# Decays of a gated linear attention made in place, level by level, and its scan begun at the keys

## The chip, the cores and the metric

The kernel runs on one core of one Trainium2 chip. Its time is device time in microseconds (us), of the one core; three runs stand for it and their median is the figure used. The engines are named as in the profile: PE (TensorE: matmuls), PEld (its weight loads), DVE (VectorE), ACT (ScalarE), POOL (GpSimd), SP (SyncE, which issues most transfers here). PE writes into PSUM, of which the kernel uses eight banks of 128 x 512 float32: three called `pj`, three `pt`, two `pc`.

## What is computed

One layer of a decoder trunk over 16 meta tokens and 2048 real ones of width 1024. From the normed input `u` one wide projection gives the inputs of two branches, an SSD branch (16 heads in 4 groups, chunks of 128) and a gated linear attention (4 heads, keys of 128, values of 256), and the gates that merge them; a branch projection and an output projection follow. The change lies in the linear attention. Cut to its core:

```python
q = q.reshape(b, l, GLA_HEADS, GLA_HEAD_K) * (GLA_HEAD_K ** -0.5)
gate_logit = jnp.einsum('blr,rk->blk', a_lr, gla_gate_w2) + gla_gate_b
log_a = jax.nn.log_sigmoid(gate_logit) / GLA_GATE_TEMP          # per token and key channel
gc = jnp.cumsum(to_chunks(log_a), axis=3)                       # within a chunk
def step(s, inp):
    qi, ki, vi, gi = inp
    o_inter = jnp.einsum('bhtk,bhkv->bhtv', qi * jnp.exp(gi), s)
    rel = gi[:, :, :, None, :] - gi[:, :, None, :, :]
    rel = jnp.exp(jnp.where(causal, rel, -jnp.inf))
    att = jnp.einsum('bhtk,bhsk,bhtsk->bhts', qi, ki, rel)
    o_intra = jnp.einsum('bhts,bhsv->bhtv', att, vi)
    k_dec = ki * jnp.exp(g_last[:, :, None, :] - gi)
    s_new = jnp.exp(g_last)[..., None] * s + jnp.einsum('bhsk,bhsv->bhkv', k_dec, vi)
    return s_new, o_inter + o_intra
```

The decay between a query at t and a key at s is different for each key channel, so `att` is not one matmul with a mask. The kernel (chunks of 128 tokens) takes it in levels: for a block of 2h tokens, the queries of its second half meet the keys of its first half, and the decay splits into a factor on the query's side and one on the key's side. Levels h = 64, 32, ... and the diagonal fill the lower triangle.

## The kernel before

The real tokens are four blocks of 512 (`BLK`). For each block the first half of the program projects eight units from `u` (`uh`, `ul`, a high and a low part): four SSD groups (`ssd_proj`), then four attention heads (`gla_proj`). Every large product is split into three matmuls (`accum`, lines 183 to 187). A head of `gla_proj` (line 605) projects queries, keys, values (two halves) and two output gates, each about one step; after every step `step()` (line 828) advances all generators that have been begun by one `yield`. So a scan's work lies on PE behind the projections of the next units, in an order written out by hand (`manual_schedule` for PE and SP, line 842). The order on DVE, ACT and POOL is planned by the tile scheduler, as is the order on PE in the second half.

`gates` (line 414) makes the log decays of all four heads of a block and, in line 445, their running sums inside each chunk, into `g_all`. `gla_scan` (line 644) is begun after a head's output gates; for the last head of the last block already after the values, and then the keys are turned later (`last`). It first makes the decayed keys `kd` (lines 660, 661) and the decayed queries `qg` (665, 666). `level_in(half)` (line 675) then makes, in tiles of its own, the two operands of a level: the running sum minus its value at the middle of the block (688), two exponentials (691, 692), times the keys (693) and, in two pieces, times the queries (695). The result `kq` is laid out so that both operands are contiguous. `level_out(half)` (line 699) multiplies them, two matmuls of 128 x 128 in plain float32 into a `pc` bank (line 703), and copies what belongs to that level into `xa` under a mask (line 710). A level's operands are made one to two levels ahead. Pairs of neighbours (level 1) and the diagonal are made by sums over channels with a matrix of ones (lines 751 to 776). `xa` holds two chunks in one tile: one in its upper, the other in its lower triangle, and lines 778 to 791 part them and turn one by a transpose (790). Then, chunk by chunk (796 to 806), values and state are applied, the state `s_gla` is carried on (802), and the output is normed, turned (816), gated (817) and stored (820).

The second half (from line 868) multiplies by the gate, branch and output weights, each product in seven partial ones (`product`, `PS`). Its first four products are put between the last steps of the first half (`between`, lines 1114 to 1123). Its operands are loaded and split on ACT and DVE (`prep_b`, lines 903 and 904; `prep_a`, 928 and 929), into memory that the first half gives back: one part when the projections have ended (`inputs.close()`), the rest when the scans have (`first.close()`).

Of the kernel before, what the change touches and what calls it, by code (L numbers as in the profile page):

```python
# [14 lines left out]
P = 128  # L15
# [6 lines left out]
GH = 4  # L22
# [5 lines left out]
NACT = 8  # L28
NC1 = 6
LEVELS = (64, 32, 16, 8, 4, 2)  # L30
NMSK = len(LEVELS) + 1
# [9 lines left out]
def trunk_kernel(ctx: ExitStack, tc: tile.TileContext, xm, xmt, w_feat, w_tok, w_zm, w_br, w_o,  # L41
# [85 lines left out]
    def bank(pool, tag):  # L127
        return mk(pool, [P, 512], F32, tag)

# [107 lines left out]
    def load_u(b):  # L237
# [54 lines left out]
        for kt in range(KT):  # L292
            xk = mk(wk, [P, META + BLK], F32, "act" if m0 else "acc", bufs=NACT if m0 else 2)[:, :tt]
# [38 lines left out]
    def late_constants():  # L332
        w2r = mk(wk, [P, META + BLK], F32, "act", bufs=NACT)[:48, :512]
# [11 lines left out]
    def new_block(b, u):  # L345
# [13 lines left out]
        o.g_all = mk(bpool, [P, GH, META + BLK], F32, "g_all")  # L359
        o.alr = mk(bpool, [P, 5, 48], F32, "alr")  # L360
# [53 lines left out]
    def gates(o):  # L414
        m0, tt, chunks, g_all = o.m0, o.tt, o.chunks, o.g_all
        ast = mk(wk, [P, META + BLK], F32R, "act", bufs=NACT)[:48, :tt]
# [10 lines left out]
        for h2 in range(0, GH, 2):  # L427
# [14 lines left out]
            for h in (h2, h2 + 1):  # L442
                nc.vector.tensor_tensor(gmt[:, h % 2, :tt], gmt[:, h % 2, :tt], g_all[:, h, :tt], op=ALU.subtract)
                for a, n in chunks:
                    nc.vector.tensor_tensor_scan(g_all[:, h, a:a + n], ones[:, :n], gmt[:, h % 2, a:a + n], 0.0,
                                                 op0=ALU.mult, op1=ALU.add)
                yield


    def ssd_proj(o, g):  # L450
# [16 lines left out]
        for j in range(4):  # L467
# [13 lines left out]
            f = mk(wk, [P, META + BLK], F32, "act", bufs=NACT)  # L481
# [123 lines left out]
    def gla_proj(o, h):  # L605
        m0 = o.m0
        t0 = T_GLA + 4 * h
        qs = mk(wk, [P, META + BLK], F32, "act", bufs=NACT)
        ps, = proj_feat(f"g{t0}", w_feat[t0], o.segs_real, o.mov)
        nc.scalar.activation(qs[:, :BLK], ps, AF.Copy, scale=QSCALE)  # L610
        yield
        kf = mk(wk, [P, META + BLK], F32, "act", bufs=NACT)
        for ps, (a, n) in zip(proj_feat(f"g{t0 + 1}", w_feat[t0 + 1], o.segs_all, o.mov), o.segs_all):
            nc.scalar.activation(kf[:, a:a + n], ps[:, :n], AF.Copy)
        yield
        vh = mk(wk, [P, NCH, 256], F32R, "tok4", bufs=NT4)
# [8 lines left out]

        last, gs = (o.b, h) == (nblk - 1, GH - 1), []
        if last:
            begin(gla_scan(o, h, qs, kf, (vh, vl), vm, gs, True))
        if m0:
            nc.scalar.activation(vm, pv5[:META, :256], AF.Copy)  # L630
        for r, ps in enumerate(pss):
            split(*[t[:, 2 * r:2 * r + 2].rearrange("p c f -> p (c f)") for t in (vh, vl)], ps)
        yield
        for j in range(2):
# [4 lines left out]
            gs.append(gg)  # L639
            yield  # L640
        if not last:
            begin(gla_scan(o, h, qs, kf, (vh, vl), vm, gs))

    def gla_scan(o, h, qs, kf, vt, vm, gs, last=False):
        m0, tt = o.m0, o.tt
        gf = o.g_all[:, h, :tt]
        gr = gf[:, m0:]
        q = qs[:, :BLK]
        k = kf[:, m0:tt]
        grc = gr.rearrange("p (c t) -> p c t", t=P)  # L650

        kd = mk(wk, [P, META + BLK], F32, "act", bufs=NACT)
        gl = mk(sm, [P, NCH + 1], F32, "gl")
        nc.scalar.activation(gl[:, :NCH], grc[:, :, P - 1], AF.Copy, scale=ITEMP)
        if m0:
            nc.scalar.activation(gl[:, NCH:], gf[:, META - 1:META], AF.Copy, scale=ITEMP)
            nc.scalar.activation(kd[:, :META], gf[:, :META], AF.Exp, scale=-ITEMP, bias=gl[:, NCH:])
        for c in range(NCH):
            cs = slice(m0 + c * P, m0 + (c + 1) * P)
            nc.scalar.activation(kd[:, cs], gf[:, cs], AF.Exp, scale=-ITEMP, bias=gl[:, c:c + 1])  # L660
        nc.vector.tensor_tensor(kd[:, :tt], kd[:, :tt], kf[:, :tt], op=ALU.mult)
        egl = mk(sm, [P, NCH], F32, "egl")
        nc.scalar.activation(egl, gl[:, :NCH], AF.Exp)
        qg = mk(wk, [P, META + BLK], F32, "act", bufs=NACT)[:, :BLK]
        nc.scalar.activation(qg, gr, AF.Exp, scale=ITEMP)
        nc.vector.tensor_tensor(qg, qg, q, op=ALU.mult)

        xa = mk(wk, [P, 2, P], F32, "c1", bufs=NC1)
        kqs = {}

        def level_in(half):
            nb = BLK // (2 * half)
            npc = P // (2 * half)

            def view(t):
                return t.rearrange("p (b two h) -> p b two h", two=2, h=half)  # L680

            def view5(t):
                return t.rearrange("p (r o b two h) -> p r o b two h", o=2, b=npc, two=2, h=half)

            ex = mk(wk, [P, BLK], F32, "sq", bufs=NSQ)
            kq = mk(wk, [P, BLK], F32, "sq", bufs=NSQ)
            ev = view(ex)
            nc.vector.tensor_tensor(
                ex.rearrange("p (b s) -> p b s", s=2 * half), gr.rearrange("p (b s) -> p b s", s=2 * half),
                view(gr)[:, :, 0, half - 1:half].to_broadcast([P, nb, 2 * half]), op=ALU.subtract)  # L690
            nc.scalar.activation(ev[:, :, 0], ev[:, :, 0], AF.Exp, scale=-ITEMP)
            nc.scalar.activation(ev[:, :, 1], ev[:, :, 1], AF.Exp, scale=ITEMP)
            nc.vector.tensor_tensor(view(kq)[:, :, 0], ev[:, :, 0], view(k)[:, :, 0], op=ALU.mult)
            for i in range(2):
                nc.vector.tensor_tensor(view5(kq)[:, :, 1 - i, :, 1], view5(ex)[:, :, i, :, 1],
                                        view5(q)[:, :, i, :, 1], op=ALU.mult)
            kqs[half] = kq

        def level_out(half):
            kq = kqs.pop(half)  # L700
            ps = bank(pc, "pc")
            for r in range(2):
                nc.tensor.matmul(ps[:, r * P:(r + 1) * P], kq[:, 2 * r * P:(2 * r + 1) * P],
                                 kq[:, (2 * r + 1) * P:(2 * r + 2) * P], start=True, stop=True)
            pv2 = ps[:, :256].rearrange("p (r t) -> p r t", t=P)
            if half == 64:
                nc.scalar.activation(xa, pv2, AF.Copy)
            else:
                mi = msk[:, LEVELS.index(half)].unsqueeze(1).to_broadcast([P, 2, P])
                nc.vector.copy_predicated(xa, mi, pv2)  # L710

        level_in(64)
        yield
        if m0:
            ps = bank(pt, "pt")
            nc.tensor.transpose(ps[:META, :P], kd[:, :META], ident)
            btm = mk(wk, [P, P], F32, "bt")
            nc.scalar.activation(btm[:META], ps[:META, :P], AF.Copy)
        kdt = []

        def turn_keys():
            ps = bank(pt, "pt")
            for c in range(NCH):
                nc.tensor.transpose(ps[:, c * P:(c + 1) * P], kd[:, m0 + c * P:m0 + (c + 1) * P], ident)
            kdt.extend(mk(wk, [P, NCH, P], F32R, "kdt", bufs=2) for _ in range(2))
            split(*[t.rearrange("p c t -> p (c t)") for t in kdt], ps)

        if not last:
            turn_keys()
        level_in(32)  # L730
        level_out(64)
        level_in(16)
        yield
        if m0:
            ps = bank(pc, "pc")
            nc.tensor.matmul(ps[:, :256], btm[:META], vm, start=True, stop=True)
            nc.vector.tensor_copy(s_gla[:, h], ps[:, :256])
        level_out(32)
        level_in(8)
        level_out(16)  # L740
        level_in(4)
        yield
        level_out(8)
        level_in(2)
        level_out(4)


        def halves(t):
            return t.rearrange("p (r o b two) -> p r o b two", o=2, b=P // 2, two=2)

        pn = mk(wk, [P, 2, P // 2, 2], F32, "c1", bufs=NC1)
        for i in range(2):
            eo = pn[:, :, :, 1 - i]
            nc.vector.tensor_tensor(eo, halves(gr)[:, :, i, :, 1], halves(gr)[:, :, i, :, 0], op=ALU.subtract)
        nc.scalar.activation(pn, pn, AF.Exp, scale=ITEMP)
        for i in range(2):
            eo = pn[:, :, :, 1 - i]
            nc.vector.tensor_tensor(eo, eo, halves(q)[:, :, i, :, 1], op=ALU.mult)
            nc.vector.tensor_tensor(eo, eo, halves(k)[:, :, i, :, 0], op=ALU.mult)
        pd = mk(wk, [P, BLK], F32, "sq", bufs=NSQ)  # L760
        nc.vector.tensor_tensor(pd, q, k, op=ALU.mult)
        parts = []
        for src, n, tg, nb in ((pn.rearrange("p r b o -> p (r b o)"), 256, "c1", NC1), (pd, BLK, "sq", NSQ)):
            hl = [mk(wk, [P, n], F32R, tg, bufs=nb) for _ in range(2)]
            split(*hl, src)
            parts.append((hl, n))
        yield
        level_out(2)
        sums_ = []
        for hl, n in parts:  # L770
            ps = bank(pt, "pt")
            for i in range(2):
# [460 lines left out]
```

## Time and profile before

| | us |
|---|---|
| median of three runs | 2326.85 |
| the runs | 2323.31, 2326.85, 2329.19 |
| the profiled execution, its span | 2327.3 |
| busy PE, PEld | 2247.1, 1956.3 |
| busy DVE, ACT, POOL | 1550.3, 1184.8, 684.6 |

The profiled execution is known by its span alone, from its first to its last instruction; no time outside the span is given for it. Matmuls are pipelined: the start of one to the start of the next tells what it costs, the duration of one is longer. A float32 matmul shows as two records, each with its weight load; so four records of line 703 are one level. "[2.59 <-ACT junk L806]" behind an instruction of a timeline is the time its engine stood idle before it and what ended that. In a group's row stand the instruction's line, engine and operation, what it writes and reads, the count, then the busy time, the mean ns of one, and the idle time before it with its cause.

### The profile page before, as it was taken

To read this page: it belongs to the slowest core of one execution; us is meant where nothing else is said; L and a number is where in the kernel's file an instruction comes from. 1 tells how busy PE (TensorE), PEld (TensorE's weight loads), DVE (VectorE), ACT (ScalarE), POOL (GpSimd) and SP (SyncE) were. 2 spreads that over 40 slices of the span, in tenths; PEclk is the share of its full clock that TensorE was granted. 3 is DMA by queue.
4 is the path that set the end of the run, shared out by engine and by line. 5 is a ranking of instruction groups with operands and counts; after the bars stand their busy time and mean duration, and the time that the engine had idled before them with its cause. 6 is when DMAs were issued, how large, how long until landed. Compare 5 with 4: busy or idle time off the path is not lost. (4 is left out here: it accounts for less than half of the span.)

```text
span 2327.3 us, 36519 instructions
## 1 busy us (share of the span) xinstructions
PE 2247.1 (97%) x12641; PEld 1956.3 (84%) x12641; DVE 1550.3 (67%) x2895; ACT 1184.8 (51%) x2758; POOL 684.6 (29%) x681
## 2 busy tenths in 40 slices
PE   7899999999999999999999999889999999999998
PEld 7899888888888989898988898768888888888776
DVE  5676766676675666566568555654588954788766
ACT  4666655465544455544465443554554545554443
POOL 3344433122221122212122100037324264324331
PEclk9999999999999999999999999989999999999999
DMA  8766865767785666786677655457577866687743
GB/s 302 230 204 208 292 228 205 223 199 237 244 284 181 214 213 217 255 270 215 194 230 214 206 168 162 145 178 247 186 255 268 305 227 216 231 286 259 243 145 122
DMA packets 301545, 518.05 MB, mean 223 GB/s; under 512 B 27696, under 2 KB 143664, under 8 KB 301360
## 3 DMA queue, kind: packets, MB, share of 16 engines
q1 hardware_dynamic: 200400, 402.84, 53.0%
q10 hardware_dynamic: 100960, 112.88, 14.1%
q8 instruction: 99, 1.62, 0.3%
q14 instruction: 86, 0.70, 0.1%
HBM read 368.42 MB, written 147.19 MB: 222 GB/s over the span
## 5 line engine op out<-in xcount | busy, mean ns | idle before, releaser
L185 PE MATMUL pj<-u,whl 128*128 128x512 f32 (+1 forms) x1184 | 449.0, 379 | 14.6 <-ACT acc L475 6.7
L187 PE MATMUL pj<-u,whl 128*128 128x512 f32 (+1 forms) x1184 | 433.5, 366 | 1.4 <-POOL whl L166 0.8
L186 PE MATMUL pj<-u,whl 128*128 128x512 f32 (+1 forms) x1184 | 432.0, 365 | 0.0
L185 PE MATMUL pj<-whl,u 128*128 128x256 f32 (+1 forms) x992 | 289.0, 291 | 2.4 <-ACT u L298 1.5
L187 PE MATMUL pj<-whl,u 128*128 128x256 f32 (+1 forms) x992 | 282.4, 285 | 1.6 <-DVE u L300 1.6
L186 PE MATMUL pj<-whl,u 128*128 128x256 f32 (+1 forms) x992 | 282.2, 284 | 1.0 <-POOL whl L166 1.0
L185 PEld LDWEIGHTS pj<-u,whl 128*128 128x128 f32 x1184 | 226.8, 192 | 53.7 <-ACT acc L475 7.7
L185 PE MATMUL pj<-b,a 128*128 128x512 f32 x640 | 254.0, 397 | 13.8 <-ACT sn L945 7.6
L187 PEld LDWEIGHTS pj<-u,whl 128*128 128x128 f32 x1184 | 226.0, 191 | 38.0 <-POOL whl L166 1.9
L186 PEld LDWEIGHTS pj<-u,whl 128*128 128x128 f32 x1184 | 227.0, 192 | 33.6
L187 PE MATMUL pj<-b,a 128*128 128x512 f32 x640 | 252.2, 394 | 0.0
L186 PE MATMUL pj<-b,a 128*128 128x512 f32 x640 | 251.0, 392 | 0.0
L185 PEld LDWEIGHTS pj<-whl,u 128*128 128x128 f32 x992 | 189.7, 191 | 4.0 <-ACT u L298 1.8
L187 PEld LDWEIGHTS pj<-whl,u 128*128 128x128 f32 x992 | 189.6, 191 | 2.3 <-DVE u L300 2.3
L80 POOL TENSOR_TENSOR wr<-wr 128x256 f32<-128x256 f32 x80 | 66.3, 829 | 425.0 <-DMA wr<-u 174.7
L186 PEld LDWEIGHTS pj<-whl,u 128*128 128x128 f32 x992 | 189.9, 191 | 1.6 <-POOL whl L166 1.2
L166 POOL TENSOR_TENSOR whl<-wr,whl 128x512 fp32r<-128x512 f32 (+1 forms) x100 | 134.7, 1355 | 187.4 <-ACT whl L165 151.5
L904 DVE TENSOR_TENSOR b<-br,b 128x512 fp32r<-128x512 f32 x196 | 154.9, 808 | 44.7 <-ACT b L903 43.5
L919 POOL TENSOR_TENSOR as<-ar,ar 128x512 f32<-128x512 f32 x40 | 60.0, 1499 | 411.3 <-DMA ar<-in_w_br 197.3
L479 DVE SCALAR_TENSOR_TENSOR acc<-cin,hcw,acc 128x512 f32<-128x512 f32 (+1 forms) x192 | 154.4, 804 | 30.9 <-ACT acc L475 29.8
L929 DVE TENSOR_TENSOR a<-ar,a 128x512 fp32r<-128x512 f32 x160 | 126.3, 797 | 67.2 <-ACT a L928 64.4
L903 ACT ACTIVATE b<-br 128x512 fp32r<-128x512 f32 x196 | 119.4, 626 | 99.0 <-DMA br<-br_t 38.6
(274 smaller groups left out, 5068.8 us busy)
## 6 DMA issues: line engine op xcount, KB each, us to landing
whl<-k_s SPq DMA_DIRECT2D x96, 512.0 KB, 4.5
whl<-k_g SPq DMA_DIRECT2D x96, 512.0 KB, 4.2
whl<-k_v SPq DMA_DIRECT2D x48, 512.0 KB, 3.7
whl<-k_z SPq DMA_DIRECT2D x36, 512.0 KB, 3.8
wr<-in_w_feat SPq DMA_DIRECT2D x64, 256.0 KB, 4.5
k_s<-whl SPq DMA_DIRECT2D x32, 512.0 KB, 3.6
cb<-cumd ACTq DMA_DIRECT2D x64, 256.0 KB, 5.8
y<-gg ACTq DMA_DIRECT2D x64, 256.0 KB, 4.5
```

What stands on the lines that cost most here:

```text
L80: nc.gpsimd.tensor_tensor(o, x, y, op=ALU.subtract)
L166: nc.gpsimd.tensor_tensor(hl[:, 1], raw, hl[:, 0].bitcast(F32), op=ALU.subtract)
L185: nc.tensor.matmul(ps, sh, mh, start=first, stop=False, **kw)
L186: nc.tensor.matmul(ps, sh, ml, start=False, stop=False, **kw)
L187: nc.tensor.matmul(ps, sl, mh, start=False, stop=last, **kw)
L479: nc.vector.scalar_tensor_tensor(acc, cin[:, k:k + tt], hcw[:, ti, k:k + 1], acc, op0=ALU.mult, op1=ALU.add)
L903: nc.scalar.activation(t[:, 0], raw, AF.Copy)
L904: nc.vector.tensor_tensor(t[:, 1], raw, t[:, 0].bitcast(F32), op=ALU.subtract)
L919: nc.gpsimd.tensor_tensor(s1, a21, a22, op=ALU.add)
L929: nc.vector.tensor_tensor(t[:, 1], src, t[:, 0].bitcast(F32), op=ALU.subtract)
```

## The change

- `gates` leaves the log decays themselves in `g_all`; the running sums inside a chunk are gone.
- Keys and queries of a head are halves of one tile (`pair_tile`, four of two rows each in place of eight single ones; other users of that pool take halves too). The scan is begun right after the keys' projection (`gla_keys`); the values and the output gates come into lists that the scan reads later.
- The scan sums the log decays over blocks of 2, 4, ... 128 tokens, and takes the exponentials of all of them at once. It starts with queries that carry their own token's decay, and goes from level 1 up to level 64. After a level, `level(half)` multiplies keys and queries in place: the keys of a block's first half and the queries of its second half by the exponential of the other half's sum. After level 64 they are the keys decayed to the chunk's end and the queries decayed from its start, which `kd` and `qg` were.
- A level's stationary operand is packed by ACT into a tile of its own (`pack`); the moving operand is read with strides straight from the pair tile (`odd_even`), in runs of `half` elements that alternate between keys and queries. There are seven levels by matmul; the sums over channels remain for the diagonal alone. The chunks that share `xa` are now 0 with 2 and 1 with 3.
- In the last block, the keys of head 3 are projected before the output gates of head 2. A scan has fourteen steps where it had eleven.
- Tile counts: `NACT` 8 to 4 (of double size), `NC1` 6 to 7.

```diff
-NACT = 8
-NC1 = 6
-LEVELS = (64, 32, 16, 8, 4, 2)
+NACT = 4
+NC1 = 7
+LEVELS = (1, 2, 4, 8, 16, 32, 64)
...
+    def pair_tile(dt=F32):
+        return mk(wk, [P, 2, META + BLK], dt, "act", bufs=NACT)
...
-                nc.vector.tensor_tensor(gmt[:, h % 2, :tt], gmt[:, h % 2, :tt], g_all[:, h, :tt], op=ALU.subtract)
-                for a, n in chunks:
-                    nc.vector.tensor_tensor_scan(g_all[:, h, a:a + n], ones[:, :n], gmt[:, h % 2, a:a + n], 0.0,
-                                                 op0=ALU.mult, op1=ALU.add)
+                nc.vector.tensor_tensor(g_all[:, h, :tt], gmt[:, h % 2, :tt], g_all[:, h, :tt], op=ALU.subtract)
...
+    def gla_keys(o, h):
+        kq = pair_tile()
         ps, = proj_feat(f"g{t0}", w_feat[t0], o.segs_real, o.mov)
+        nc.scalar.activation(kq[:, 1, m0:m0 + BLK], ps, AF.Copy, scale=QSCALE)
+        yield
         for ps, (a, n) in zip(proj_feat(f"g{t0 + 1}", w_feat[t0 + 1], o.segs_all, o.mov), o.segs_all):
+            nc.scalar.activation(kq[:, 0, a:a + n], ps[:, :n], AF.Copy)
+        o.gla[h] = [], []
+        begin(gla_scan(o, h, kq, *o.gla[h]))
+        yield
...
+    def gla_proj(o, h):
+        ahead = o.b == nblk - 1 and h >= GH - 2
+        if not ahead or h == GH - 2:
+            yield from gla_keys(o, h)
+        yield from gla_values(o, h)
+        if ahead and h == GH - 2:
+            yield from gla_keys(o, GH - 1)
+        yield from gla_out_gates(o, h)
...
+        def odd_even(half, start, nb, skip):
+            pitch = list(kq.ap[0])
+            return bass.AP(kq.tensor, kq[:, 0, start:].offset, [pitch, [2 * half, nb], [skip, 2], [1, half]])
...
+        while n > NCH:
+            n //= 2
+            dst = ex[:, at:at + n]
+            two = src.rearrange("p (b two) -> p b two", two=2)
+            nc.vector.tensor_tensor(dst, two[:, :, 0], two[:, :, 1], op=ALU.add)
+            place[BLK // n] = (at, n)
+            src, at = dst, at + n
+        nc.scalar.activation(ex[:, :BLK], la, AF.Exp, scale=ITEMP)
+        nc.scalar.activation(egl, src, AF.Exp, scale=ITEMP)
+        nc.scalar.activation(ex[:, BLK:at - NCH], ex[:, BLK:at - NCH], AF.Exp, scale=ITEMP)
+        nc.vector.tensor_tensor(pd, q, k, op=ALU.mult)
+        nc.vector.tensor_tensor(q, q, ex[:, :BLK], op=ALU.mult)
...
+        def pack(half):
+            packed[0] = mk(wk, [P, 2 * P], F32, "c1", bufs=NC1)
+            nb = P // half
+            nc.scalar.activation(packed[0].rearrange("p (b two h) -> p b two h", two=2, h=half),
+                                 odd_even(half, m0, nb, k_to_q + 2 * P + half), AF.Copy)
+
+        def level(half):
             ps = bank(pc, "pc")
             for r in range(2):
+                nc.tensor.matmul(ps[:, r * P:(r + 1) * P], packed[0][:, r * P:(r + 1) * P],
+                                 odd_even(half, m0 + (r + 2) * P, P // (2 * half), k_to_q - 2 * P + half),
+                                 start=True, stop=True)
...
+            nb = BLK // (2 * half)
+            kv = odd_even(half, m0, nb, k_to_q + half)
+            at = place[half][0]
+            other = bass.AP(ex.tensor, ex[:, at + 1:].offset, [list(ex.ap[0]), [2, nb], [-1, 2], [0, half]])
+            nc.vector.tensor_tensor(kv, kv, other, op=ALU.mult)
+            if half < P // 2:
+                pack(2 * half)
```

More of the change, by code (lines that the diff above doesn't have):

```diff
@@ L292, in load_u @@
         for kt in range(KT):
-            xk = mk(wk, [P, META + BLK], F32, "act" if m0 else "acc", bufs=NACT if m0 else 2)[:, :tt]
+            if not m0:
+                xk = mk(wk, [P, META + BLK], F32, "acc")[:, :tt]
+            else:
+                if kt % 2 == 0:
+                    two = pair_tile()
+                xk = two[:, kt % 2, :tt]
             nc.sync.dma_start(xk, xmt[:, kt, row0:row0 + tt])
@@ L638, in gla_proj @@
             nc.vector.scalar_tensor_tensor(gg, gg, 1.0, ps, op0=ALU.add, op1=ALU.mult)
-            gs.append(gg)
+            o.gla[h][1].append(gg)
             yield
-        if not last:
-            begin(gla_scan(o, h, qs, kf, (vh, vl), vm, gs))
-    def gla_scan(o, h, qs, kf, vt, vm, gs, last=False):
-        m0, tt = o.m0, o.tt
[L646 to L654, printed above, removed]
-        if m0:
[L656 to L666, printed above, removed]
-        xa = mk(wk, [P, 2, P], F32, "c1", bufs=NC1)
[L673 to L700, printed above, removed]
@@ L715, in gla_scan @@
             ps = bank(pt, "pt")
-            nc.tensor.transpose(ps[:META, :P], kd[:, :META], ident)
+            nc.tensor.transpose(ps[:META, :P], km, ident)
             btm = mk(wk, [P, P], F32, "bt")
             nc.scalar.activation(btm[:META], ps[:META, :P], AF.Copy)
[L719 to L732, printed above, removed]
+        level(2)
+        yield
+        level(4)
         yield
@@ L760, in gla_scan @@
[L760 to L772, printed above, removed]
-                nc.tensor.matmul(ps[:, :n], ones_r, hl[i], start=i == 0, stop=i == 1)
-            sums_.append(ps)
@@ L775, in gla_scan @@
-        nc.vector.copy_predicated(xa, msk[:, len(LEVELS)].unsqueeze(1).to_broadcast([P, 2, P]),
-                                  sums_[0][:, :256].rearrange("p (r t) -> p r t", t=P))
+        level(16)
+        yield
+        level(32)
+        pdt = [mk(wk, [P, BLK], F32R, "sq", bufs=NSQ) for _ in range(2)]
+        split(*pdt, pd)
+        yield
+        level(64)
+        diag = bank(pt, "pt")
+        for i in range(2):
+            nc.tensor.matmul(diag, ones_r, pdt[i], start=i == 0, stop=i == 1)
@@ L1189, in _layout @@
     cmsk[:, 0] = np.eye(P)
-    for i, h in enumerate(LEVELS + (1,)):
+    for i, h in enumerate(LEVELS):
         if i:
```

89 lines of the change are left out of this document (47 added, 42 removed).

## The prediction

> **What bounds the kernel now.** I read the page's busy shares first, then the busy times by stretch, then what TensorE (PE) waited for, then PE's timeline where the stretches show a hole.
>
> ```profile
> PE 2247.1 (97%) x12641; PEld 1956.3 (84%) x12641; DVE 1550.3 (67%) x2895; ACT 1184.8 (51%) x2758; POOL 684.6 (29%) x681
> ```
>
> PE is busy 97% of a span of 2327.3 us. The profiled execution is 0.45 us above the median shown (2326.85), so a sum made against the span may be read against the median. Only 80 us of PE idle time exist, and what the change takes from VectorE (DVE) and ScalarE (ACT) is worth nothing but the part of those 80 us that it frees. So I need to know where they lie.
>
> ```profile
> 965.00:1012.00 47.00, 43.53 (x270) 38.69 (x269) 29.48 (x69) 26.16 (x74) 12.60 (x17) 1.00 0.78 260
> ...
> 1190.00:1240.00 50.00, 49.73 (x299) 42.95 (x298) 37.31 (x77) 32.35 (x78) 11.28 (x17) 1.00 0.67 204
> ...
> 1367.00:1407.00 40.00, 40.00 (x246) 35.84 (x245) 20.12 (x50) 14.04 (x33) 1.76 (x2) 1.00 0.52 169
> ...
> 1450.00:1494.00 44.00, 44.00 (x275) 39.45 (x274) 26.65 (x71) 20.51 (x57) 2.19 (x1) 1.00 0.38 125
> 1494.00:1523.00 29.00, 18.82 (x89) 15.42 (x88) 24.29 (x50) 16.45 (x43) 8.59 (x6) 0.76 0.50 164
> 1523.00:1536.00 13.00, 13.00 (x65) 10.95 (x64) 2.90 (x6) 6.05 (x19) 3.56 (x4) 1.00 0.00 0
> 1536.00:1550.00 14.00, 7.90 (x27) 6.12 (x26) 9.95 (x15) 7.61 (x14) 1.22 (x1) 0.76 0.73 249
> ```
>
> Columns: stretch, its length, then busy PE, PEld, DVE, ACT, POOL, the granted clock, DMA. The first four are linear-attention heads and one SSD group; PE hardly stops there. From 1494 to 1550, between the last input projection and the steady products of the second half, PE idles 16 us and the granted clock falls to 0.76, while DVE is busy 24.29 of 29 us.
>
> ```profile
> PE pt L790 <- DVE sq L781: 6.8, 2, 4.4
> PE pj L185 <- ACT acc L475: 6.7, 5, 4.3
> PE pc L801 <- DVE s_gla L802: 6.6, 6, 2.7
> PE pj L185 <- ACT b L903: 6.1, 1, 6.1
> PE pj L185 <- ACT g_all L437: 4.4, 2, 3.1
> PE pc L703 <- ACT junk L806: 3.7, 2, 2.6
> PE pc L564 <- DVE sq L555: 3.5, 2, 2.6
> ```
>
> Columns: total, times, longest. L703 (levels) and L790 (transposes of the attention blocks) are the only waits on the decays that the change rewrites; their longest, 2.6 and 4.4 us, and the 6.1 us, stand in the hole:
>
> ```profile
> 1493.77 0.38 PE L790 MATMUL pt<-cst,sq 128*128 128x128 f32 x2
> ...
> 1502.34 2.51 PE L703 MATMUL pc<-sq 128*128 128x128 f32 x8 [2.59 <-ACT junk L806]
> ...
> 1516.78 0.66 PE L790 MATMUL pt<-cst,sq 128*128 128x128 f32 x2 [4.42 <-DVE sq L781]
> ...
> 1518.80 0.56 PE L185 MATMUL pc<-tok,kdt 128*128 128x256 f32 x1
> ...
> 1522.74 0.59 PE L185 MATMUL pj<-b,a 128*128 128x512 f32 x1
> ...
> 1536.19 1.04 PE L816 MATMUL pt<-cst,ot 128*128 128x128 f32 x8
> 1543.32 1.22 PE L185 MATMUL pj<-b,a 128*128 128x512 f32 x2 [6.10 <-ACT b L903]
> ...
> 1549.33 0.39 PE L186 MATMUL pj<-b,a 128*128 128x512 f32 x1
> 1549.56 0.40 PE L187 MATMUL pj<-b,a 128*128 128x512 f32 x1
> ```
>
> The last projection ends at 1493.77. The last two scans then run with little cover: the first product starts 29.0 us later, the four early products (48 matmuls) last till 1536.19, the last output transposes follow, and the next products (p = 6) start at 1543.32, 49.55 us after the projection. They run slowly at first: 14 matmuls from 1543.32 to 1549.33, 0.43 us apart where the next two rows stand 0.23 apart, a loss of 2.8 us. So this passage costs 52.3 us.
>
> **The change, part by part.** *The levels on PE.*
>
> ```profile
> 1486.68 0.60 PE L703 MATMUL pc<-sq 128*128 128x128 f32 x4
> 1487.04 0.48 PE L773 MATMUL pt<-c,ones_r 128*128 128x256 f32 x2
> 1487.36 0.63 PE L773 MATMUL pt<-sq,ones_r 128*128 128x512 f32 x2
> 1487.83 0.61 PE L703 MATMUL pc<-sq 128*128 128x128 f32 x4
> 1488.19 0.47 PE L185 MATMUL pj<-u,whl 128*128 128x512 f32 x1
> ```
>
> Sixteen scans each get a seventh level and lose the column sum of neighbours (128x256). A level takes 0.36 us from start to next start (1486.68 to 1487.04, and 1487.83 to 1488.19), that sum 0.32 us: 16 x (0.36 - 0.32) = +0.6 us. All else on PE is the same work in another order.
>
> *The moving operand with strides.* Before, a level's two operands were written contiguous; now the stationary one is packed by ACT and the moving one is read from keys and queries in runs of 1, 2, ... 64 elements. No matmul of this trace reads so. Bounds: nothing, since a level of four records of 128 columns takes 0.36 us, 0.09 each, while 512 columns pass in 0.23 us, 0.06 per 128, so reading is not what paces it; or each level doubles, 16 x 7 x 0.36 = +40 us. Nearest rows are those of the same runs on other engines:
>
> ```profile
> L695 DVE TENSOR_TENSOR sq<-sq,act x192: 276/285/1391, 255.2 to 1504.2; 128x128 f32<-128x128 f32 x192
> ```
>
> Runs from 64 down to 2 elements are in this group, with shortest 276 and median 285 ns: the run's length does not show. I take 0. A run of 1 that alternates between keys and queries is in no row; if that level alone doubles: 16 x 0.36 = +5.8 us. [...]
>
> *DVE and ACT.*
>
> ```profile
> L688 DVE TENSOR_TENSOR sq<-g_all 128x512 f32<-128x512 f32 x96 | 75.6, 787 | 0.5
> L695 DVE TENSOR_TENSOR sq<-sq,act 128x128 f32<-128x128 f32 x192 | 54.6, 325 | 0.0
> L693 DVE TENSOR_TENSOR sq<-sq,act 128x256 f32<-128x256 f32 x96 | 45.5, 474 | 6.2 <-PE pc L703 4.8
> L710 DVE COPY_PREDICATED c<-msk,pc 128x256 f32<-128x256 uint8 x80 | 35.5, 444 | 41.1 <-PE pc L703 41.1
> L445 DVE TENSOR_TENSOR_SCAN g_all<-ones_r,tok 128x128 f32<-128x128 f32 x64 | 22.9, 417 | 0.0
> ```
>
> Gone: 75.6 + 54.6 + 45.5 + 22.9 = 198.6 us. New: 112 in-place multiplications of 512 elements at 0.787 = 88 us, and 112 block sums, at most 16 x 0.474 + 96 x 0.325 = 39 us. DVE is relieved by some 70 us over the first half, ACT by less. Off PE's path this is hidden already (PE had 40 of 40 us in 1367 to 1407), so I cost it at nothing. The one place where DVE's relief can count is the gates and the SSD features beside them (11.1 us of waits on L475 and L437 above, of which DVE's prefix scans may be part): I take -2, bounds 0 and -11.
>
> *The chain that the change adds.* Before, a level's operands were made two levels ahead. Now level 2h needs level h's matmul read, the masked copy (0.444), the multiplication in place (0.787) and ACT's pack, which has 256 elements as the half exponentials have:
>
> ```profile
> L691 ACT ACTIVATE sq<-sq 128x256 f32<-128x256 f32 x96 | 40.3, 420 | 109.7 <-DVE sq L688 97.0 <-POOL wr L80 11.8 <-DVE sq L695 0.7
> ```
>
> That is 0.444 + 0.787 + 0.42 = 1.65 us, some 2.5 with three hand-overs, in a step of 40/6 = 6.7 us (one of six projection steps of a head). The nearest chain that exists is masked copies, product and copy before L790: it waits 6.8 - 4.4 = 2.4 us over the 15 covered scans. Seven such links per scan at that rate give 16.8 us, the upper end; shorter links with two thirds of a step to spare give 0. I take +3. Behind a waiting level stands the next projection on PE's queue, so each wait counts in full. Buffers: keys and queries now hold pairs; a late pair delays ACT's evacuation first and PE only after the three pj banks fill. I cost it at nothing; if that cover is gone, one wait like L475's 4.3 us per block.
>
> *The scan begun at the keys and the last head's keys ahead.* The last scan now starts six steps before the projections end, so seven of its fourteen steps are left. After the last projection, PE's order is: two chunks of head 2, two levels (32 and 64), the diagonal sum, head 2's output transposes, the key and attention transposes, four chunks, two products, the last output transposes, two products. A chunk's price:
>
> ```profile
> 1200.81 0.29 PE L185 MATMUL pc<-tok,kdt 128*128 128x256 f32 x1
> ...
> 1201.77 0.47 PE L185 MATMUL pc<-tok,kdt 128*128 128x256 f32 x1
> ```
>
> 0.96 us covered; 3.94/2 = 1.97 in the hole (1518.80 to 1522.74). The sum from the end of the projection: chunks 1.9 and the wait for a pc bank as now, 2.6 (to 4.5); level 32 and its link 0.4 + 2.5, level 64 0.5 (to 7.9); masked copy, causal product, diagonal copy, two splits and transposes, about 5.2 by their sizes (0.44 per 256 and 0.7 per 512 elements) with hand-overs (to 13.1); four chunks at 1.97 (to 21.0); 24 matmuls at 0.23 (to 26.5); transposes 1.0; 24 matmuls (to 33.0); slow clock 1.5: 34.5 us. What of the loads?
>
> ```profile
> 1505.93 7.04 SPq L898 DMA_DIRECT2D br<-u  x4
> 1537.25 11.75 SPq L898 DMA_DIRECT2D br<-gate_t  x11
> ```
>
> The four operands of product 2 are issued by 19.2 us after the projection, before their product; the gate loads on SP's queue start 1.06 us after the last output transposes start, and p = 6 starts 6.1 after that, both from 1536.19. With the transposes at 26.5 this gives 33.7, now beside 24 matmuls. So 34.5 stands: 52.3 - 34.5 = 17.8 us. What moved ahead of the projection's end is PE work there: three levels (1.1), two chunks (1.9), one pair of transposes (0.2): 3.2 us. Net -14.6, with ends -4 (only the bank and attention waits shrink, 2.6 + 4.4 less 3.2) and -20.
>
> **Sum.** 2327.3 - 14.6 + 0.6 - 2 + 3 + 0 = 2314.3; I say 2314.
>
> **The rivals.** (a) *The level chain becomes the wait* (slower). Place: each block's first linear-attention head, where the scan now overlaps SSD's last scan. There DVE has 29.48 of 47 us already, and the scan's first six steps add some 10 us (block sums 39/16 = 2.4, two products of 0.787, five levels of 0.444 + 0.787): about 84%. For: L564 waited up to 2.6 us on DVE in that overlap. Against: at 37.31 of 50 us (75%) PE lost 0.27 us. Twenty levels (5 x 4 blocks) decide at 13/20, some 0.65 us of wait per level; at 1.5 us the time is 2314 + 30 = 2344, at 2.6 us 2366. (b) *The strided read paces PE*: level 1 only, 2314 + 6 = 2320; all levels, 2354. Against: 0.09 against 0.06 us above. (c) *The change shortens no path*: the hole is kept by the loads and by ACT's and DVE's order in it, the first product comes no sooner than its operands and the 4 us end holds: 2327.3 - 4 + 1.6 = 2325. For: DVE is 84% busy there, with the second half's splits also. Against: the waits named are on the scan's own tiles.
>
> **How the numbers follow.** Forecast 0.53, (a) 0.21, (b) level 1 only 0.05, all levels 0.04, (c) 0.17. 0.3% (7 us, about what this kernel's runs can tell) puts the forecast with faster: 0.53; (c) and level 1 only with same: 0.22; (a) and all levels with slower: 0.25. The forecast's own range is 2302 to 2320 (tail -20 to -9 or so). The range to 2345 takes in (c), (b) level 1 and half of (a), leaving out some 0.15 above and 0.05 below.
>
> **What would show it.** Right: from the last projection to the p = 6 products some 35 us instead of 49.55, no ACT b wait of 6 us, DVE's busy time down by 70 us or more, PE idle near 65 us. Each level near 0.36 us back to back. Wrong: a line of waits of PE's pc levels on ACT c (the pack) with many times; a level 1 that takes 0.7 us; a passage of 45 us or more whose longest wait is on the loads or on L903's successor.

## The result and the profile after

The changed kernel takes 2356.49 us (median of 4 runs, 2353.7 to 2356.76); the kernel before, run beside it, 2328.02 us. The ratio is 1.011 with a 95% interval of 1.0087 to 1.0133: slower by 28 us, where 14 us less were forecast. The time lies above the range. The profiled execution has a span of 2355.0 us, 27.7 more than before. In this document a kernel's line numbers are its own: after the change a level's matmuls are L712, the chunk's product with the state is L786, and ACT's pack is L706.

The busy shares on the page of the kernel after:

```profile
PE 2261.0 (96%) x12673; PEld 1963.7 (83%) x12673; DVE 1450.1 (62%) x2547; ACT 1143.9 (49%) x2582; POOL 678.5 (29%) x681
```

DVE is relieved by 100 us and PE, which has nearly the same work (32 records more of 12673), is 14 us longer busy and 14 us longer idle. What PE waited for, kernel after (total, times, longest):

```profile
PE pc L712 <- DVE s_ssd L578: 12.3, 7, 4.0
...
PE pj L188 <- ACT acc L481: 7.7, 5, 5.4
PE pc L786 <- DVE s_gla L787: 6.7, 4, 2.6
PE pc L712 <- DVE c L583: 5.2, 5, 1.5
PE pc L712 <- ACT c L706: 5.0, 1, 5.0
...
PE pj L188 <- ACT g_all L446: 3.3, 2, 3.1
...
PE pc L188 <- ACT kdt L236: 3.1, 1, 3.1
...
PE pj L188 <- ACT b L888: 2.4, 1, 2.4
```

The first line was not there before. A level waits 12 times, 17.5 us in all, for L578 and L583. These are no instructions of the attention scan: they are SSD's, the addition that takes a chunk's state out of its `pc` bank, and the one that takes the chunk's output out of the other. The pack, the last link of the chain that I had priced, holds PE up once. PE's timeline where the last block's first head runs beside SSD's last scan, kernel after:

```profile
1383.01 0.49 PE L548 MATMUL pt<-cst,act 128*128 128x128 f32 x3
1383.34 1.00 PE L572 MATMUL pc<-c,sq 128*128 128x64 f32 x8
1384.18 0.65 PE L573 MATMUL pc<-s_ssd,act 128*128 128x256 f32 x2
1384.67 0.59 PE L575 MATMUL pc<-c,bt 128*128 128x256 f32 x2
1386.88 0.72 PE L712 MATMUL pc<-act,c 128*128 128x128 f32 x4 [1.62 <-DVE s_ssd L578]
1387.34 0.48 PE L188 MATMUL pj<-u,whl 128*128 128x512 f32 x1
```

SSD takes one `pc` bank for its output (L572, L573) and the other for its state (L575). There are only two. The level stands directly behind, needs a bank, and stops PE's queue until the state has been added: 2.21 us from L575 to the level. The next projection stands behind the level and waits with it. Before the change no attention scan was begun here, and a projection, which writes into `pj`, followed SSD's state product (L567 in the kernel before):

```profile
1368.52 0.59 PE L567 MATMUL pc<-c,bt 128*128 128x256 f32 x2
1368.77 0.58 PE L185 MATMUL pj<-u,whl 128*128 128x512 f32 x1
```

Where the 27.7 us arose, from the starts of PE's matmuls (after less before): the last input projection ends 42.1 us later (1535.90 against 1493.77); from there to the first product of p = 6 it takes 39.85 us instead of 49.55, which leaves 32.4; another 4.7 come back behind that.

To see where the 42.1 lie I divided PE's time up to the last projection matmul into two parts. An insertion is a run of matmuls that are not projections; its cost is the time from its first start to the start of the second projection matmul behind it, less that matmul's steady pace (0.227 us for 512 columns, 0.12 for 256). The rest belongs to the projections. Kernels of the experiments below are in the same table:

| us | before | after | levels in `pt` (e1) | SSD state in `pt` (e5) | young first (e8) | before, young first (e9) |
|---|---|---|---|---|---|---|
| start of the last projection matmul | 1493.5 | 1535.7 | 1515.7 | 1510.7 | 1490.2 | 1497.1 |
| all insertions | 354.1 | 398.6 | 382.3 | 374.2 | 366.0 | 369.5 |
| the projections | 1139.4 | 1137.1 | 1133.4 | 1136.5 | 1124.2 | 1127.6 |
| 16 insertions with an SSD chunk and a level | none | 73.9 | 54.6 | 47.5 | 43.5 | none |

The insertions cost 44.5 us more than before. The 16 places where a level and an SSD chunk stand together (four in each block's first head) cost 73.9 us, and the same matmuls cost 43.5 us where nothing in them waits for a bank. So 30.4 of the 44.5 us arise at this one collision. Not all of it is waiting for a bank. PE stands idle for 23.7 us in the 16 places: 20.0 us until DVE has emptied one (17.5 before a level, 2.5 before the product of the meta tokens' state, L744), and 3.2 us until an operand of SSD is ready (L563), which the kernel before had as well (3.5 us, on L555). In the rest PE works, but more slowly; two of the places, with their levels at 633.27 and 1005.79, reach into stretches with a granted clock of 0.50 (631.80 to 638.60 and 1000.40 to 1010.60).

The passage at the end of the projections, kernel after:

```profile
1535.90 0.28 PE L188 MATMUL pc<-tok,kdt 128*128 128x256 f32 x1
...
1538.64 0.71 PE L712 MATMUL pc<-act,c 128*128 128x128 f32 x4
1544.33 1.22 PE L712 MATMUL pc<-act,c 128*128 128x128 f32 x4 [4.98 <-ACT c L706]
...
1552.79 0.39 PE L188 MATMUL pc<-tok,kdt 128*128 128x256 f32 x1 [3.13 <-ACT kdt L236]
...
1561.17 0.58 PE L188 MATMUL pj<-b,a 128*128 128x512 f32 x1
...
1566.83 1.03 PE L801 MATMUL pt<-cst,ot 128*128 128x128 f32 x8
...
1575.75 0.73 PE L188 MATMUL pj<-b,a 128*128 128x512 f32 x2 [2.41 <-ACT b L888]
```

It is shorter, as meant, by 9.7 us: the first product starts 25.3 us after the projection (29.0 before), and p = 6 at 39.85.

### The profile page after: what moved, and what is told of

Its sections match the earlier page's. It is cut to its first block, busy times and chain, and to the rows that moved or that the text cites. A ratio compares the mean times of both kernels' runs of the same rounds, so it can differ in the third digit from the quotient of the medians.

```text
span 2355.0 us, 35946 instructions
## 1 busy us (share of the span) xinstructions
PE 2261.0 (96%) x12673; PEld 1963.7 (83%) x12673; DVE 1450.1 (62%) x2547; ACT 1143.9 (49%) x2582; POOL 678.5 (29%) x681
```

## The experiments

The theory from this profile: a level's place on PE's queue is behind instructions that hold both `pc` banks, so it is the bank that is waited for (bank theory). The rival that I had named: the chain of masked copy, multiplication and pack is too long for its step (chain theory). And the strided read was still without a price.

**e1: the levels take their bank from `pt`, which has three.**

```diff
         def level(half):
-            ps = bank(pc, "pc")
+            ps = bank(pt, "pt")
```

> The levels take their PSUM bank from the three pt banks instead of the two pc banks; nothing else changes. Bank theory (a level stands on PE right behind the SSD state products or the chunk products, which hold both pc banks until DVE and ACT have read them): the level's waits on DVE s_ssd (12.3 us), DVE c L583 (5.2 us) and the slow hand-overs behind the chunks (about 0.3 us each, 21 of them) go; the time falls by 15 to 28 us, to 2329 to 2342. Chain theory (the copy, multiplication and pack between two levels are late because DVE is loaded in the overlap): the same levels wait as long, now on ACT's pack or on DVE, and the time stays within 6 us of 2356.

Measured: 2335.52 us, ratio to before 1.0036 [1.0021, 1.0052]: 21 us less than the change as it was made. The waits on L578 and L583 at the levels are gone. The timeline at the same kind of place, e1:

```profile
1384.30 1.00 PE L572 MATMUL pc<-c,sq 128*128 128x64 f32 x8
1385.14 0.65 PE L573 MATMUL pc<-s_ssd,act 128*128 128x256 f32 x2
1385.62 0.59 PE L575 MATMUL pc<-c,bt 128*128 128x256 f32 x2
1386.06 0.61 PE L712 MATMUL pt<-act,c 128*128 128x128 f32 x4
1386.42 0.48 PE L188 MATMUL pj<-u,whl 128*128 128x512 f32 x1
```

0.44 us from L575 to the level instead of 2.21. The operands are the same, made by the same chain at the same place in the program, and they were there in time. The 16 insertions fall from 73.9 to 54.6 us. It is still no gain over before.

**e2: three `pc` banks and two `pt` banks**, with the levels in `pc` as after.

```diff
-    pt = ctx.enter_context(tc.tile_pool(name="pt", bufs=3, space=bass.MemoryType.PSUM))
-    pc = ctx.enter_context(tc.tile_pool(name="pc", bufs=2, space=bass.MemoryType.PSUM))
+    pt = ctx.enter_context(tc.tile_pool(name="pt", bufs=2, space=bass.MemoryType.PSUM))
+    pc = ctx.enter_context(tc.tile_pool(name="pc", bufs=3, space=bass.MemoryType.PSUM))
```

> Three pc banks and two pt banks in place of two and three; the levels stay in pc. Bank theory: the waits behind the SSD state products go as in the run with the levels in pt, since a third bank is free when the level comes; 2329 to 2345 unless new waits on pt (transposes) cost as much, which would show as waits of PE pt. Chain theory: 2350 to 2362, waits now on ACT's pack.

Measured: 2353.94 us, 1.0123 [1.0093, 1.0152], no better than after. PE's waits, e2:

```profile
PE pt L418 <- DVE kdt L237: 6.3, 3, 2.1
PE pt L406 <- DVE tkc L402: 6.1, 3, 2.3
...
PE pt L735 <- DVE kdt L237: 3.9, 3, 1.3
```

No level waits for SSD any more, and the 16 insertions fall to 46.0 us, but a small product and a transpose of SSD's decays (L406, L418) and the transpose of the meta tokens' keys (L735), which use `pt`, now wait for its two banks. The shortage was moved. The three pools hold eight banks together in all these kernels, and no run had a ninth; within the eight a bank for the levels has to come from a better share or from a better order.

**e3: the last head's keys not ahead.**

```diff
-        ahead = o.b == nblk - 1 and h >= GH - 2
+        ahead = False
```

> The last head's keys are projected in their usual place again, after head 2's output gates; all else as in the changed kernel. If the passage at the end of the projections gave 14 us back, as the landmarks of the two traces say (42 us behind at the last projection, 28 us at the end), the time rises to 2366 to 2374 and the last scan has two more steps behind the projections. If that recovery came only from the shorter DVE work in the passage, the time stays within 4 us of 2356.

Measured: 2364.44 us, 1.0167 [1.0138, 1.0195], 8 us more than after and just under the range that was expected. The last projection ends 33.5 us later than before instead of 42.1, and the passage takes 49.21 us, as before (49.55). So the shorter passage is due to the keys ahead alone, and what they move in front of the projections' end costs 8.6 us there. At p = 6 that is almost a draw (33.2 against 32.4 us behind the kernel before); by these two profiles the gain of the part is the 4.7 us behind it, which e3 does not have.

**e4: level 1's moving operand packed by ACT too.**

```diff
+            if half == 1:
+                mov1[0] = mk(wk, [P, 2 * P], F32, "c1", bufs=NC1)
+                nc.scalar.activation(mov1[0].rearrange("p (b two h) -> p b two h", two=2, h=half),
+                                     odd_even(half, m0 + 2 * P, nb, k_to_q - 2 * P + half), AF.Copy)
...
+                                 mov1[0][:, r * P:(r + 1) * P] if half == 1 else
                                  odd_even(half, m0 + (r + 2) * P, P // (2 * half), k_to_q - 2 * P + half),
```

> For level 1 alone the moving operand is packed by ACT too, so that PE reads it contiguous. If a run of one element slows PE's read, level 1 behind the diagonal sum falls from 0.52 us from start to next start to 0.36, 16 x 0.16 = 2.6 us in all; if the 0.52 is the change from one kind of matmul to the other, it stays at 0.52. The whole time moves by less than can be told.

Measured: one execution, 2347.96 us; what it was run for is the duration of level 1. Level 64 of an older head, the diagonal sum and level 1 of a younger one stand in a row, kernel after:

```profile
1467.95 0.61 PE L712 MATMUL pc<-act,c 128*128 128x128 f32 x4
1468.31 0.71 PE L757 MATMUL pt<-sq,ones_r 128*128 128x512 f32 x2
1468.86 0.82 PE L712 MATMUL pc<-act,c 128*128 128x128 f32 x4
1469.38 0.42 PE L188 MATMUL pj<-whl,u 128*128 128x256 f32 x1
```

And e4 (L716 is the level, `c` its dense moving operand):

```profile
1417.44 0.61 PE L716 MATMUL pc<-act,c 128*128 128x128 f32 x4
1417.81 0.72 PE L762 MATMUL pt<-sq,ones_r 128*128 128x512 f32 x2
1418.36 0.61 PE L716 MATMUL pc<-c,c 128*128 128x128 f32 x4
1418.72 0.36 PE L188 MATMUL pj<-whl,u 128*128 128x256 f32 x1
```

From start to next start level 1 takes 0.52 us when it reads single elements out of keys and queries in turn (1468.86 to 1469.38), and 0.36 us when it reads a packed tile (1418.36 to 1418.72). Level 64 takes 0.36 us in both, and levels with runs of two elements or more take 0.36 to 0.39 us (behind a chunk 0.44 to 0.47 in the kernel after, and 0.47 in the one such place of the kernel before, whose operands are contiguous; in e8, where levels 4 and 8 stand ahead of the chunks, 0.36 again). So the price of the strided read is 0.16 x 16 = 2.6 us, all of it in level 1.

**e5: the levels in `pc` as after, but SSD's state product in `pt`.**

```diff
-            pst = bank(pc, "pc")
+            pst = bank(pt, "pt")
             nc.tensor.matmul(pst[:, :256], bt, xw.rearrange("p a c -> p (a c)"), start=True, stop=True)
```

> The levels stay in the two pc banks; the SSD scan's state product takes a pt bank instead. So a level behind it finds a pc bank free, but behind the chunks of an older attention scan it does not. Bank theory: the waits on DVE s_ssd and c L583 before levels go, those on ACT's reads of the chunks' banks stay; the time falls by 10 to 20 us, to 2336 to 2347. If it was the number of instructions on DVE in the overlap, nothing moves: 2350 to 2360.

Measured: 2336.73 us, 1.0023 [1.0009, 1.0038]. No level waits for L578 or L583, and the 16 insertions take 47.5 us. Taking the other party out of the two banks is worth as much as taking the level out: it is the pair of them that costs, not the level's own work. A level behind a chunk of an older scan still shares `pc` here, and those 20 insertions cost what they cost after (70.7 us against 69.3; 64.2 in e1). That is another 5 us which moving the level to `pt` saves; that the bank is their cause is not shown further, for in e8 below, where the level goes first, they cost 69.3 us again.

**e6: e1 and e4 together**, with block 0's levels left in `pc`.

```diff
-            ps = bank(pc, "pc")
+            ps = bank(pc, "pc") if m0 else bank(pt, "pt")
```

> Levels in pt from the second block on, in pc in the first (where the run with all levels in pt waited 3.3 us on the meta keys' transposes), and level 1 with a contiguous moving operand. By the rows: 2335.5, less 16 x 0.16 = 2.6 for level 1, less some 4 for the first block: 2329, 2325 to 2334. This is the candidate that would reach the kernel before.

Measured: 2332.89 us, 1.0009 [0.9996, 1.0021]. Both repairs of resources together bring the change back to the time of the kernel before, not below it.

**e7: e1 with a longer chain.** After each in-place multiplication DVE multiplies the same elements once more, by one; the result is the same.

```diff
             nc.vector.tensor_tensor(kv, kv, other, op=ALU.mult)
+            nc.vector.tensor_scalar(kv, kv, 1.0, None, op0=ALU.mult)
```

> Levels in pt, and after each in-place multiplication one more DVE instruction that multiplies keys and queries by one, so that the chain between two levels has one link more. Chain theory: with no slack each of 15 x 6 links adds its 0.5 to 0.8 us, 45 to 70 us, and PE waits on ACT c L707 in number. Bank theory: the step hides it; within 6 us of 2335.5.

Measured: 2337.04 us, 1.0022 [1.0004, 1.004], the same as e1. DVE's busy time rises from 1458.8 to 1493.6 us, 0.31 us in each of the 112 links, and PE does not feel it: its waits on L706 are 4.0 us once in e1, 5.4 us in two times here. The chain has room to spare behind the projections, and the chain theory falls.

**e8: the changed kernel with the generators advanced from the youngest to the oldest.** With the scan begun at the keys, the scan that hands out levels is always younger than the SSD scan or the attention scan whose chunks run beside it.

```diff
     def step():
...
-        for gen in list(running):
+        for gen in list(running)[::-1]:
```

> In every step the scans begun last go first, so that a level stands on PE ahead of the SSD state product and ahead of an older scan's chunks, with all banks as in the changed kernel. Bank theory: the level finds banks that were read a step ago, and the SSD products behind it wait for the level's masked copy instead, which is shorter; the time falls by 5 to 20 us from 2356, and waits of the SSD products on DVE c (the masked copy) appear. If it is the load on DVE and not the order, the time stays within 5 us of 2356.

Measured: 2313.11 us, 0.9926 [0.9901, 0.9951]: 43 us less than after with the same instructions, and 18 us less than the kernel before. The same overlap of the last block, e8:

```profile
1341.15 0.65 PE L712 MATMUL pc<-act,c 128*128 128x128 f32 x4
1341.64 0.49 PE L548 MATMUL pt<-cst,act 128*128 128x128 f32 x3
1341.96 1.00 PE L572 MATMUL pc<-c,sq 128*128 128x64 f32 x8
1342.80 0.65 PE L573 MATMUL pc<-s_ssd,act 128*128 128x256 f32 x2
1343.29 0.59 PE L575 MATMUL pc<-c,bt 128*128 128x256 f32 x2
1343.53 0.58 PE L188 MATMUL pj<-u,whl 128*128 128x512 f32 x1
```

The level comes first, when DVE's last reading of a `pc` bank (L583, to 1336.62) lies 4.5 us back, and behind L575 stands a projection, which starts 0.24 us later. From the first of these starts to the projection's it is 2.38 us; in the kernel after the same matmuls, with the level last, take 4.33 (1383.01 to 1387.34). The table shows what the rest of the gain is: insertions 32.6 us less than after, 30.4 of them in the 16 places; the projections 12.9 us less; and the passage 34.3 us instead of 39.85. The fall is more than twice the 20 us that were expected at most, and the waits of SSD's products for the masked copy that were expected do not appear: PE is nowhere idle in the 16 places.

**e9: the same line in the kernel before.**

```diff
-        for gen in list(running):
+        for gen in list(running)[::-1]:
```

> The kernel before, with the same reversal in every step: the scans begun last go first. If the order helps only because a level stood behind the SSD state product, which it does not in the kernel before (its first head's levels begin when SSD's last scan has ended), the time stays within 7 us of 2328. If the order is worth some 20 us by itself (the SSD stages gained 5 us per block in the changed kernel with it), the time falls to 2305 to 2318, and then the change in place, with this order, is worth nothing more.

Measured: 2330.4 us, 1.0007 [0.9991, 1.0023]. The order by itself is worth nothing there. PE's waits, e9:

```profile
PE pc L801 <- DVE s_gla L802: 15.7, 19, 3.0
```

By the table the projections gain 11.8 us here as well, but the insertions lose 15.4: in the kernel before, a chunk that no longer runs first waits for the state of the chunk ahead (15.7 us of such waits against 6.6, so 9.1 more). In e8 the same kind of wait (L786 on L787) is 9.3 us in 23 times. So it is the change and the order together that are faster.

**e10: e8 with level 1 dense as in e4. e11: e10 with the levels in `pt`.** Both are e8 with edits shown above.

> The changed kernel with scans begun last first, and level 1 with a contiguous moving operand. Behind the diagonal sum or a projection, level 1 falls by 0.16 us: 2313 - 2.6 = 2310.5, 2306 to 2315. ACT has 16 packs more, which cost nothing on PE if the pack has slack, as the longer chain had.

> As the last, and the levels in pt banks. With the order reversed no level waits behind the state product any more, so the bank theory sees nothing left to win: 2305 to 2316, equal to the last within 5 us. If the pc banks still cost something (0.4 us hand-overs behind chunks, SSD products behind a level), it falls by more than 5 us below the last.

Measured: 2315.5 us, 0.9949 [0.9931, 0.9967], and 2314.76 us, 0.9951 [0.9934, 0.9969]. Neither differs from e8 by more than the runs spread (2307.95 to 2319.05), and e10 lies just above its range. Where levels stand ahead of the bank holders, another bank pool was worth nothing; and 2.6 us of PE time that e10 saves can't be told from the spread.

## Why the prediction was wrong, point by point

*The step that failed* is the sentence on buffers: I considered the pair tiles and `pj`, and "cost it at nothing". I never counted who holds the two `pc` banks at the moment when a level comes up in its new place. The rows were there to be read: the program's order puts the new scan behind SSD's in each `step()`, SSD's chunk takes one `pc` bank and then the other, and my own table of waits showed a level stopped on `pc` by an older scan's chunk ("PE pc L703 <- ACT junk L806"). This cost 19 to 30 us in the first heads (73.9 us against 54.6 in e1, 47.5 in e5 and 43.5 in e8), and some 5 more behind older chunks if e1 is the measure (69.3 against 64.2).

*The chain, +3.* It measured nothing in the covered scans: PE never waited for the pack there, and another 0.31 us per link changed no time (e7). The 0.85 us for three hand-overs in the 2.5 us of a link was an estimate of mine that stood on no row. In the kernel after a covered link takes 1.51 us from the level's end to the pack's (1417.93 to 1419.44), with 0.03 us from PE to DVE and 0.03 from DVE to ACT.

*Rival (a)* had the right place (each block's first head, beside SSD's last scan), the right sign and nearly the right size (2344 to 2366; measured 2356), with a chance of 0.21. Its mechanism, DVE's load, was wrong in the main. It put DVE at 84% in the first head of the third block. In the kernel after that stretch has DVE busy for 29.20 of 47 us (999 to 1046), which is 62%, and the last block's first head, where the timeline above lies, 57% (its length, then busy PE, PEld, DVE, ACT, POOL, clock, DMA):

```profile
1369.00:1408.00 39.00, 34.85 (x219) 30.70 (x219) 22.21 (x50) 13.82 (x40) 3.73 (x5) 1.00 0.40 125
```

In e1 and e8 DVE has the same work (1458.8 and 1454.3 us busy against 1450.1), and these waits are gone. What DVE has in hand at the moment does set how long a wait is. At the place of the timeline, DVE in the kernel after:

```profile
1385.14 0.93 DVE L237 TENSOR_TENSOR sq<-sq,sq 128x512 fp32r<-128x512 f32 x1
1385.99 0.41 DVE L580 TENSOR_TENSOR c<-pc,ecu 128x256 f32<-128x256 f32 x1
1386.33 0.40 DVE L578 TENSOR_TENSOR s_ssd<-s_ssd,pc 128x256 f32<-128x256 f32 x1
```

SSD's matmuls end at 1385.26. DVE first finishes a split of the younger attention scan (L237), which takes 0.8 us more, before it comes to SSD's banks. The same stands in two of the other places (645.80 and 1018.11). So there DVE lengthens the wait by up to 0.8 us; the level's place behind the two banks makes it.

*The scan begun at the keys and the keys ahead, -17.8 gross.* Right in kind, and mis-sized: the forecast for this passage, without the slow clock behind it, was 33.0 us against 49.55, and it took 39.85, a gain of 9.7. By the steps of the sum: the last level done at 9.3 us instead of 7.9 (with the pack's wait of 4.98 us: from level 32 to level 64 it takes 5.7 us, 1538.64 to 1544.33, where 2.9 were counted, so here, without cover, the chain was priced too low); the first chunk at 16.9 instead of 13.1 (the keys are turned and split only there, and the 3.13 us on L236 are that split); the four chunks 8.4 instead of 7.9; and 14.6 instead of 12.0 from the first product to p = 6. In e8 the passage takes 34.3 us, close to the forecast. Work moved ahead of the projections' end cost 8.6 us (e3) where I had counted 3.2. By the same division as in the table the insertions take 4.0 of them, close to the 3.2; the rest lies at the projections, which lose 13.7 us in stretches with a granted clock of 0.50 in the kernel after and 8.7 in e3, for a reason that is not shown.

*The seventh level, +0.6, and the strided read, 0.* Levels from 2 to 64 (0.36 to 0.39 us away from chunks) are no slower than the contiguous ones were (0.36), so their read cost nothing here, as forecast. Level 1 pays 0.16 us each, 2.6 in all, inside the bounds that I had given (0 to 5.8). So a run of one element paid and a run of two did not; what makes the difference is not shown.

*The gates, -2.* The waits on L481 and L446 are 7.7 and 3.3 us, as they were (6.7 and 4.4): nothing gained.

*DVE and ACT.* DVE's busy time fell by 100 us (70 or more forecast). No gain on PE from it shows, as forecast.

*The sum again*, in measured terms: 2327.3 + 44.5 for the insertions (30.4 at the SSD chunks, some 5 at older chunks, 2.6 for level 1, some 6 not separated) - 2.3 at the projections - 9.7 in the passage - 4.7 behind it = 2355.1, against a span of 2355.0.

*What stays open.* The projections take 12 to 13 us less when the youngest generator goes first, and the traces show where, though not why. Taken as steps between neighbouring projection matmuls, above the usual step of their size, the loss is 61.7 us in the kernel after and 49.5 in e8. Of it 13.7 us lie in stretches with a granted clock of 0.50 in the kernel after (seven before the last projection, 41.0 us long together) and 2.4 us in e8 (two, 6.8 us): 11.3 of the 12.2 us. The waits for L481 and L446 fall from 11.0 us to 3.5 as well, while 3.1 us of waiting for L481 come up at a product of the gates (L443) and small steps take the rest back. In the kernel before and e9 the loss in such stretches is 11.0 and 5.9 us. Over whole executions the granted clock is 0.986 to 0.988 in the four of the kernel after and 0.992 to 0.994 in the four of e8. That the order causes the fuller clock is not shown: e7, in the old order, has 5.6 us of such loss, and e10, in the new one, 6.0. So some 11 of the 49 us between these two profiled executions (43 between the medians) are clock, and their cause is open. To begin head 0's scan later, so that it does not meet SSD's scan at all, was not tried.

## What to carry to other kernels

When a step is moved in an order written out by hand, ask of each resource that it takes, and of shared PSUM banks above all, who holds them at the new place and which instruction of which engine gives them back; a wait there was paid by what stood behind it too (2.21 us from L575 to the level, and the projection came only after it, at 1387.34). Where two interleaved generators share a small pool, the one whose product is short and whose result is needed soon goes ahead of the one that fills the pool: here that one line was worth 43 us in the changed kernel, where another use of the banks was worth 21 at most; part of that, some 11 us by the two profiles, is a fuller clock, whose cause is not shown. A change that loses in one order can win in another (2356 and 2313 us with the same instructions), so the order belongs to the change.

## What the runs showed of the hardware

Level 1, two float32 matmuls of 128 columns whose moving operand goes from keys to queries and back with each element, took 0.52 us to the next start, and 0.36 with that operand packed (e4); the levels with runs of two elements or more took 0.36 to 0.39 unpacked, away from chunks. The step from SSD's state product in plain float32 (L575) to the next start was 0.24 us where a projection of 512 columns followed (kernel after, median of 28; 1343.29 to 1343.53 in e8), and 0.43 and 0.44 us where a level that waited for nothing did (e1, 1377.94 to 1378.37 and 1385.62 to 1386.06). But the projection's first matmul then took 0.42 us to its next start instead of 0.23 (the same 28; 1343.53 to 1343.95 in e8), so the cost was only shifted; a price read from one row's start to the next must take in the first matmul behind it.
